# Small products of the first mixer issued in one visit of the array, modulation weights by two chunks

## The chip, the cores and the metric

The kernel runs on one core of a Trainium2 chip. The metric is the device time in microseconds of one execution. Before the change three runs took 1012.62, 1013.31 and 1016.01 us; the median is 1013.31. Engines are named as in the profile: PE is the matrix engine, DVE the vector engine, ACT the scalar engine, SP the queue that issues most loads.

## The reference, cut to what matters

One inference step of a two-layer transformer-like trunk over 384 tokens (128 context tokens, 256 latent tokens) of width 1024. Each layer computes six modulation vectors from a conditioning vector, then a mixer, then a feed-forward network. The change concerns the mixer of layer 0:

```
mod = silu(cond) @ w_mod[l] + b_mod[l]            # 1024 -> 6 x 1024: shift, scale, gate, twice
u   = layer_norm(x) * (1 + sc1) + sh1
# mixer of layer 0: projections of u, then
#   windowed attention, 8 query heads on 2 key/value heads:
s = q @ k^T / 8, masked;  p = softmax([s, sink]);  wo = p @ v
#   bidirectional retention, 8 heads (rv: values, s0: a state from the cache):
o = (q k^T * decay) @ rv + (q * decay) @ s0
x = layer_norm(ALPHA * x + g1 * ([ret, wo] @ w_out))
```

The feed-forward network behind it (1024 to 2816 and back) takes most of the time and isn't touched.

## The kernel before, in words

Everything is in float32; large products run as three products of rounded and rest parts (`r_...`, `l_...` for weights, `ur`, `ul` for activations). Weight tiles of 512 KB are loaded by the SP queue into a ring of five raw tiles (`raw_unit`, line 162), then ACT copies the rounded part and DVE subtracts for the rest part (`split`, line 172). The modulation weights use the same ring but no split: PE multiplies them straight from the raw tile.

The tokens are tiled by 128 (`NB` = 3 blocks). The first mixer consists of projections in slabs (`rqk`, `rvg`, each a stretch of 128 by 512 matmuls), twelve window items (three blocks by four head pairs), the retention of two halves, and modulation steps 2, 3 and 4 of layer 0. A string of steps (`AORDER`, line 33) sets the order in which the code emits these; a scheduler then places instructions on each engine by priority and by when it takes operands to be ready. `hmm` and `boost` (lines 116 and 120) raise the priority of a small product by 600, so it slips in between the matmuls of a projection as soon as its operand is due. `tc.issue_after(op)` adds an order edge only: what is emitted inside it comes behind `op` on its engine.

Three functions matter. `mod_pe` (line 223) takes eight chunks of the contraction. Each is one load `rawm` and four products, each on a column tile of 32 of the array. `win1` (line 855) makes the scores `ws` of an item and their exponentials `wp` for both heads (q = 0, 1). `win2` (line 884) normalises `wp`, transposes it on PE (`tw`), copies it on ACT (`wpT`), multiplies it with the values (`wpo`, six products for an item of blocks 1 and 2 and two for one of block 0, on column tiles of 64) and writes the rounded and rest parts (`catr` on ACT, `catl` on DVE, `cat_split`, line 388). `av_sample` (line 1044) is the retention's output: products of weights `at` with values `rv` and of `gm` with the state `s0`, accumulated in `po`. In the trace a product in float32 shows as two matmuls, so a chunk of modulation has eight and a long item's `wpo` twelve; `mod`, `wpo` and the other small products all carry line 118, a projection line 377.

A run of small products of one tile shape that PE takes without another shape between is called a visit here.

Of the kernel before, what the change touches and what calls it, by code (L numbers as in the profile page):

```python
# [19 lines left out]
P = 128  # L20
D = 1024
NB = 3
KC = 8
# [41 lines left out]
def trunk_kernel(ctx: ExitStack, tc: tile.TileContext, a: dict):  # L65
    nc = tc.nc
    mm = nc.tensor.matmul
    V, S, G, SY = nc.vector, nc.scalar, nc.gpsimd, nc.sync
# [41 lines left out]
    def big(shape, name):  # L110
        return perm.tile(shape, F32, tag="s", name=name, bufs=4)
# [4 lines left out]
    def boost(f, *args, **kw):  # L116
        with tc.high_priority(offset=BOOST):
            return f(*args, **kw)  # L118

    def hmm(*args, **kw):  # L120
        return boost(mm, *args, **kw)
# [13 lines left out]
    ident = const.tile([P, P], F32, name="ident")  # L135
# [11 lines left out]
    cmod = const.tile([P, KC, 32], F32, name="cmod")  # L147
# [14 lines left out]
    def raw_unit(src, shape, name):  # L162
        t = perm.tile([P] + shape, F32, tag="raw", name=name, bufs=5)
        SY.dma_start(t, src)
        return t
# [48 lines left out]
    def mod_tile(l, v):  # L214

        bm = perm.tile([P, 256], F32, tag="bm", name=f"bm{l}_{v}", bufs=2)
        if v in (2, 5):
            bsrc = a["b_mod"][l, v * D : (v + 1) * D].rearrange("(j n) -> j n", j=4)
            for j in range(4):
                S.dma_start(bm[32 * j : 32 * j + 32, :], bsrc[j : j + 1, :].broadcast_to([32, 256]))  # L220
        return bm

    def mod_pe(l, v, ps, hmm=hmm):
        w = a["w_mod"][l].rearrange("(p k) n -> p k n", k=KC)
        bm = mod_tile(l, v)
        for k in range(KC):
            t = raw_unit(w[:, k, v * D : (v + 1) * D], [D], f"rawm{l}_{v}_{k}")
            for j in range(4):
                hmm(ps[32 * j : 32 * j + 32, 0:256], cmod[:, k, :], t[:, j * 256 : (j + 1) * 256],
                    start=(k == 0), stop=(k == KC - 1))  # L230
        if v in (2, 5):
            V.tensor_tensor(bm, ps[:, 0:256], bm, ALU.add)
        else:
            V.tensor_copy(bm, ps[:, 0:256])
        return bm
# [146 lines left out]
    def transpose_to(dst, srcs, pt):  # L382
        n = len(srcs)
        for i, s_ in enumerate(srcs):
            boost(nc.tensor.transpose, pt[:, i * P : (i + 1) * P], s_, ident)
        S.copy(dst, pt[:, 0 : n * P].rearrange("p (n t) -> p n t", n=n))
# [431 lines left out]
    def mixer_ab(u, cat, early, early_es, ap, ap_es, pto, mt, gm, wkT, wv, wqT, mods):  # L818
# [15 lines left out]
        bk = Banks("pab", S=1, M=1, X=1)  # L834
# [3 lines left out]
        if True:  # L838
# [7 lines left out]
            s0 = big([P, 2, 4, P], "s0")  # L846
# [37 lines left out]
            def win2(b, c):  # L884
                nk = 1 if b == 0 else 3
                w = nk * P
                tiles = [0] if b == 0 else [1, 2, 3]
                kv = c // 2
                pts, es, sm = wst.pop((b, c))
                V.tensor_tensor(sm, sm, es, ALU.add)  # L890
                V.reciprocal(sm, sm)
                pTs = []
                for q, pt in enumerate(pts):
                    V.tensor_scalar(pt[:, 0:w], pt[:, 0:w], sm[:, q : q + 1], None, ALU.mult)
                    pT = ap2.tile([P, 3, P], F32, tag="pT", name=f"wpT{b}_{c}_{q}", bufs=5)
                    transpose_to(pT[:, 0:nk, :], [pt[:, i * P : (i + 1) * P] for i in range(nk)], (pto("T", f"tw{b}_{c}_{q}") if q == 0 else bk("X", f"tw{b}_{c}_{q}")))
                    pTs.append(pT)
                po = pto("O", f"wpo{b}_{c}")
                for i in range(nk):
                    for q in range(2):  # L900
                        hmm(po[64 * q : 64 * q + 64, 0:P], wv[:, tiles[i], kv * 64 : kv * 64 + 64], pTs[q][:, i, :],
                            start=(i == 0), stop=(i == nk - 1))
                cat_split(cat, 4 + c, 1, slice(b * P, (b + 1) * P), po[:, 0:P])

            items = [(b, c) for b in range(NB) for c in range(4)]
# [138 lines left out]
            def av_sample(hh, b, ats):  # L1044
                rv = half[hh][2]
                po = pto("O", f"po{hh}_{b}")
                ic = slice((b - 1) * P, b * P)
                for c in range(2):
                    for r_ in range(2):
                        hmm(po[:, 256 + c * P : 256 + (c + 1) * P], gm[hh][:, c, r_, ic], s0[:, r_, 2 * hh + c, :],  # L1050
                            start=(r_ == 0), stop=(r_ == 1))
                    for q in (2 * c, 2 * c + 1):
                        for ji in range(2):
                            hmm(po[:, q * 64 : q * 64 + 64], ats[q][:, ji, ic], rv[:, 1 + ji, q * 64 : q * 64 + 64],
                                start=(ji == 0), stop=(ji == 1))
                return ret_out(hh, b, po)

            def ret_core(hh):
# [285 lines left out]
    for l in range(2):  # L1344
        pto = Banks(f"pto{l}", T=1, O=1)
# [32 lines left out]
        hh = tuple(lnp.tile([P, NHEAD, NTOK], F32R, name=f"hh{q}{l}") for q in "rl")  # L1378
# [142 lines left out]
```

## Time and profile before

| | |
|---|---|
| median of three runs | 1013.31 us |
| the profiled execution | 1011.62 us |
| its span, first to last instruction | 1009.8 us |
| PE busy | 990.1 us, 98 % of the span, 5679 matmuls |
| DVE busy | 636.3 us, 63 % |
| ACT busy | 432.4 us, 43 % |
| stretch of the first mixer's window items, modulation and retention | about 73 to 210 us of the span |

Busy time of PE is modelled from the start of a matmul, and matmuls are pipelined: a row that lasts 0.40 us may be followed by the next row after 0.23. What a matmul costs PE is therefore read as the distance from its start to the next start. Rows of one shape that follow each other are merged into one row with their count. In the timeline, "idle before" names what ended a wait, if PE stood.

### The profile page before, as it was taken

Reading aid. Unit: us, or ns where it says so; the run is one execution under the profiler, and the core shown is the slowest. Engines: PE = TensorE matmul, PEld = TensorE weight load, DVE = VectorE, ACT = ScalarE, POOL = GpSimd, SP = SyncE. Lnnn points to the kernel's source line nnn. Section 1 sums busy time; section 2 is a strip of 40 time slices with the busy share of each in tenths; the row PEclk is TensorE's granted clock in tenths of the full one; section 3 lists DMA queues with packets and bytes.
Section 4 is the critical chain, followed back from the end, with each engine's and each line's share of the span. In section 5 each row is a group of like instructions: output and inputs, shape, how many; then the busy total and the mean of one; then the engine's idle time right before and its main releaser. Section 6 shows DMA issues by size and latency. Waiting matters only on the chain.

```text
span 1009.8 us, 14877 instructions
## 1 busy us (share of the span) xinstructions
PE 990.1 (98%) x5679; PEld 826.9 (82%) x5679; DVE 636.3 (63%) x1338; ACT 432.4 (43%) x786; POOL 1.2 (0%) x5
## 2 busy tenths in 40 slices
PE   9999999999999999999999999999999999999996
PEld 4775566688898988989987766787899999999985
DVE  5487658588795967968557577568743333335554
ACT  3395533227543333333427556554743333333410
POOL 0000000000000000000000000000000000000000
PEclk9999999999999999999999999999999999999999
DMA  9975446473896767777624333235574444444401
GB/s 304 300 204 189 148 147 196 168 255 95 281 304 219 215 212 248 220 219 226 193 83 151 99 95 94 91 122 211 180 265 145 125 124 126 123 124 126 155 21 43
DMA packets 109704, 172.86 MB, mean 171 GB/s; under 512 B 10176, under 2 KB 78272, under 8 KB 109632
## 3 DMA queue, kind: packets, MB, share of 16 engines
q1 hardware_dynamic: 106960, 170.87, 53.4%
q10 hardware_dynamic: 2672, 1.04, 0.4%
q8 instruction: 45, 0.74, 0.3%
q14 instruction: 27, 0.22, 0.1%
HBM read 167.52 MB, written 4.36 MB: 170 GB/s over the span
## 4 chain that ended last, share of the span: by engine, by line
PE 87%; DVE 5%; DMA 3%; ACT 3%; issue 1%; SPq 0%; ACTq 0%; DVEq 0%
PE dn L518 17%; PE wg L542 17%; PE wu L542 16%; PE cd L377 7%; PE wo L377 5%; PE rvg L377 4%; PE s L377 2%; PE rqk L377 2%; PE hg L377 2%; PE mod L118 2%; PE hu L377 1%; DMA rawm<-in_w_mod 1%; PE ms L118 1%; PE wpo L118 1%; PE ws L118 1%
## 5 line engine op out<-in xcount | busy, mean ns | idle before, releaser
L542 PE MATMUL wg<-ulf,r_wg 128*128 128x384 f32 x320 | 108.4, 339 | 0.0
L542 PE MATMUL wg<-urf,r_wg 128*128 128x384 f32 x320 | 108.0, 339 | 0.3 <-DVE sg L559 0.3
L542 PE MATMUL wu<-ulf,r_wu 128*128 128x384 f32 x320 | 108.2, 338 | 0.0
L542 PE MATMUL wu<-urf,r_wu 128*128 128x384 f32 x320 | 108.1, 339 | 0.0
L542 PE MATMUL wu<-urf,l_wu 128*128 128x384 f32 x320 | 108.1, 338 | 0.0
L542 PE MATMUL wg<-urf,l_wg 128*128 128x384 f32 x320 | 108.1, 338 | 0.0
L249 DVE SCALAR_TENSOR_TENSOR z<-mraw,cs,z 128x1024 f32<-128x1024 f32 x70 | 86.2, 1281 | 9.2 <-DMA mraw<-in_w_mod 8.8
L175 DVE TENSOR_TENSOR l_wg<-raw_wg,r_wg 128x1024 fp32r<-128x1024 f32 x40 | 48.7, 1224 | 67.9 <-ACT r_wg L173 67.8
L175 DVE TENSOR_TENSOR l_wd<-raw_wd,r_wd 128x1024 fp32r<-128x1024 f32 x36 | 44.1, 1225 | 53.6 <-ACT r_wd L173 53.6
L173 ACT CAST r_wd<-raw_wd 128x1024 fp32r<-128x1024 f32 x36 | 37.8, 1050 | 88.4 <-PE wu L542 40.1
L175 DVE TENSOR_TENSOR l_wu<-raw_wu,r_wu 128x1024 fp32r<-128x1024 f32 x40 | 48.6, 1223 | 39.5 <-ACT r_wu L173 39.5
L173 ACT CAST r_wg<-raw_wg 128x1024 fp32r<-128x1024 f32 x40 | 42.0, 1049 | 72.1 <-PE dn L518 29.9
L173 ACT CAST r_wu<-raw_wu 128x1024 fp32r<-128x1024 f32 x40 | 42.0, 1050 | 62.5 <-issue 23.9
L518 PE MATMUL dn<-l_wd,hr 128*128 128x512 f32 x168 | 66.6, 396 | 0.0
L518 PE MATMUL dn<-r_wd,hr 128*128 128x512 f32 x168 | 66.5, 396 | 0.0
L518 PE MATMUL dn<-r_wd,hl 128*128 128x512 f32 x168 | 66.5, 396 | 0.0
L542 PEld LDWEIGHTS wg<-urf,r_wg 128*128 128x128 f32 x320 | 60.1, 188 | 2.3 <-issue 0.8
L542 PEld LDWEIGHTS wu<-urf,r_wu 128*128 128x128 f32 x320 | 60.1, 188 | 1.6 <-ACT r_wg L173 0.8
L542 PEld LDWEIGHTS wu<-ulf,r_wu 128*128 128x128 f32 x320 | 60.1, 188 | 0.5
L542 PEld LDWEIGHTS wg<-ulf,r_wg 128*128 128x128 f32 x320 | 60.1, 188 | 0.5
L542 PEld LDWEIGHTS wg<-urf,l_wg 128*128 128x128 f32 x320 | 60.1, 188 | 0.0
L542 PEld LDWEIGHTS wu<-urf,l_wu 128*128 128x128 f32 x320 | 60.1, 188 | 0.0
(418 smaller groups left out, 2168.6 us busy)
## 6 DMA issues: line engine op xcount, KB each, us to landing
raw_wd<-in_w_down SPq DMA_DIRECT2D x44, 512.0 KB
rawm<-in_w_mod SPq DMA_DIRECT2D x40, 512.0 KB
mraw<-in_w_mod SPq DMA_DIRECT2D x40, 512.0 KB
raw_wg<-in_w_gate SPq DMA_DIRECT2D x40, 512.0 KB
raw_wu<-in_w_up SPq DMA_DIRECT2D x40, 512.0 KB
raw_cd<-in_w_in_cd SPq DMA_DIRECT2D x20, 512.0 KB
ms<-in_w_mod SPq DMA_DIRECT2D x16, 512.0 KB
raw_rqk<-in_w_in_ab SPq DMA_DIRECT2D x16, 256.0 KB
```

What stands on the lines that cost most here:

```text
L118: return f(*args, **kw)
L173: S.copy(r, t)
L175: V.tensor_tensor(lo, t, r, ALU.subtract)
L249: V.scalar_tensor_tensor(z[c], t, cs[:, c, k : k + 1], z[c], ALU.mult, ALU.add)
L377: op = mm(ps[:, col : col + width], u[pu][:, k0 + kk, b * P : (b + 1) * P], (r, lo)[pw][:, kk, :], start=(first and i == 0 and pu + pw == ...
L518: mm(acc[b, nh], h[fc][ph][:, b * P : (b + 1) * P], wrl[pw][:, nh * 512 : (nh + 1) * 512], start=(fc == 0 and ph + pw == 0), stop=(last an ...
L542: mm(ps[j][:, 0:NTOK], un[i][pw][:, k, j * P : (j + 1) * P], u2[pu][:, 4 * i + k, :], start=(i == 0 and k == 0 and pu + pw == 0), stop=(i ...
```

## The change

`mod_pe` takes chunks in pairs: both loads are issued, then the four products of the second chunk come first and the four of the first chunk behind them (an order edge after the last). `win2` normalises both heads' exponentials first; the transposes of q = 1 go ahead of those of q = 0, and an order edge ties the latter behind; the copies follow in that order; the products of the item are chained one behind the other. `av_sample` emits the products with the values first, from q = 3 down, chained, and those with the state behind them. The arithmetic is the same but for the order of some sums. `mw` (the steps 5 of both layers, in the output phase) uses `mod_pe` too.

```diff
--- before.py
+++ after.py
@@ -223,11 +223,18 @@
     def mod_pe(l, v, ps, hmm=hmm):
         w = a["w_mod"][l].rearrange("(p k) n -> p k n", k=KC)
         bm = mod_tile(l, v)
-        for k in range(KC):
-            t = raw_unit(w[:, k, v * D : (v + 1) * D], [D], f"rawm{l}_{v}_{k}")
-            for j in range(4):
-                hmm(ps[32 * j : 32 * j + 32, 0:256], cmod[:, k, :], t[:, j * 256 : (j + 1) * 256],
-                    start=(k == 0), stop=(k == KC - 1))
+        for k0 in range(0, KC, 2):
+            ts = [raw_unit(w[:, k, v * D : (v + 1) * D], [D], f"rawm{l}_{v}_{k}") for k in (k0, k0 + 1)]
+
+            def chunk(n):
+                for j in range(4):
+                    op = hmm(ps[32 * j : 32 * j + 32, 0:256], cmod[:, k0 + n, :], ts[n][:, j * 256 : (j + 1) * 256],
+                             start=(k0 == 0 and n == 1), stop=(k0 == KC - 2 and n == 0))
+                return op
+
+
+            with tc.issue_after(chunk(1).ins):
+                chunk(0)
         if v in (2, 5):
             V.tensor_tensor(bm, ps[:, 0:256], bm, ALU.add)
         else:
@@ -889,17 +896,28 @@
                 pts, es, sm = wst.pop((b, c))
                 V.tensor_tensor(sm, sm, es, ALU.add)
                 V.reciprocal(sm, sm)
-                pTs = []
                 for q, pt in enumerate(pts):
                     V.tensor_scalar(pt[:, 0:w], pt[:, 0:w], sm[:, q : q + 1], None, ALU.mult)
+
+                pTs = {}
+                behind = nullcontext()
+                for q in (1, 0):
                     pT = ap2.tile([P, 3, P], F32, tag="pT", name=f"wpT{b}_{c}_{q}", bufs=5)
-                    transpose_to(pT[:, 0:nk, :], [pt[:, i * P : (i + 1) * P] for i in range(nk)], (pto("T", f"tw{b}_{c}_{q}") if q == 0 else bk("X", f"tw{b}_{c}_{q}")))
-                    pTs.append(pT)
+                    tp = pto("T", f"tw{b}_{c}_{q}") if q == 0 else bk("X", f"tw{b}_{c}_{q}")
+                    with behind:
+                        for i in range(nk):
+                            op = boost(nc.tensor.transpose, tp[:, i * P : (i + 1) * P], pts[q][:, i * P : (i + 1) * P], ident)
+                    S.copy(pT[:, 0:nk, :], tp[:, 0 : nk * P].rearrange("p (n t) -> p n t", n=nk))
+                    behind = tc.issue_after(op.ins)
+                    pTs[q] = pT
                 po = pto("O", f"wpo{b}_{c}")
+                behind = nullcontext()
                 for i in range(nk):
                     for q in range(2):
-                        hmm(po[64 * q : 64 * q + 64, 0:P], wv[:, tiles[i], kv * 64 : kv * 64 + 64], pTs[q][:, i, :],
-                            start=(i == 0), stop=(i == nk - 1))
+                        with behind:
+                            op = hmm(po[64 * q : 64 * q + 64, 0:P], wv[:, tiles[i], kv * 64 : kv * 64 + 64], pTs[q][:, i, :],
+                                     start=(i == 0), stop=(i == nk - 1))
+                        behind = tc.issue_after(op.ins)
                 cat_split(cat, 4 + c, 1, slice(b * P, (b + 1) * P), po[:, 0:P])
 
             items = [(b, c) for b in range(NB) for c in range(4)]
@@ -1045,14 +1063,18 @@
                 rv = half[hh][2]
                 po = pto("O", f"po{hh}_{b}")
                 ic = slice((b - 1) * P, b * P)
-                for c in range(2):
-                    for r_ in range(2):
-                        hmm(po[:, 256 + c * P : 256 + (c + 1) * P], gm[hh][:, c, r_, ic], s0[:, r_, 2 * hh + c, :],
-                            start=(r_ == 0), stop=(r_ == 1))
-                    for q in (2 * c, 2 * c + 1):
-                        for ji in range(2):
-                            hmm(po[:, q * 64 : q * 64 + 64], ats[q][:, ji, ic], rv[:, 1 + ji, q * 64 : q * 64 + 64],
-                                start=(ji == 0), stop=(ji == 1))
+                behind = nullcontext()
+                for q in range(3, -1, -1):
+                    for ji in range(2):
+                        with behind:
+                            op = hmm(po[:, q * 64 : q * 64 + 64], ats[q][:, ji, ic], rv[:, 1 + ji, q * 64 : q * 64 + 64],
+                                     start=(ji == 0), stop=(ji == 1))
+                        behind = tc.issue_after(op.ins)
+                with behind:
+                    for c in range(2):
+                        for r_ in range(2):
+                            hmm(po[:, 256 + c * P : 256 + (c + 1) * P], gm[hh][:, c, r_, ic], s0[:, r_, 2 * hh + c, :],
+                                start=(r_ == 0), stop=(r_ == 1))
                 return ret_out(hh, b, po)
 
             def ret_core(hh):
```

The order of instructions on PE shows the window item of block 2, head pair 2. `tw` are transposes, `wpo` the output products, `mod0_3` modulation step 3, `rvg0_1` a projection. Before:

```order
L118 MATMUL tw2_2_0_1579<-ident_69,wp2_2_0_1529 128x128 x3
L118 MATMUL tw2_2_1_1586<-ident_69,wp2_2_1_1531 128x128 x3
L377 MATMUL rvg0_1_1165<-r_rvg0_1_1102,ul0_91 128x512
L118 MATMUL wpo2_2_1591<-wpT2_2_0_1578,wv_648 64x128
L377 MATMUL rvg0_1_1165<-l_rvg0_1_1103,ur0_90 128x512
L118 MATMUL wpo2_2_1591<-wpT2_2_1_1585,wv_648 64x128
L118 MATMUL wpo2_2_1591<-wpT2_2_0_1578,wv_648 64x128
L118 MATMUL wpo2_2_1591<-wpT2_2_1_1585,wv_648 64x128
L118 MATMUL wpo2_2_1591<-wpT2_2_0_1578,wv_648 64x128
L118 MATMUL wpo2_2_1591<-wpT2_2_1_1585,wv_648 64x128
```

After the change, at the same item:

```order
L118 MATMUL tw2_2_1_1580<-ident_69,wp2_2_1_1531 128x128 x3
L118 MATMUL tw2_2_0_1586<-ident_69,wp2_2_0_1529 128x128 x3
L118 MATMUL mod0_3_1625<-rawm0_3_3_1641,cmod_82 32x256 x3
L118 MATMUL mod0_3_1625<-rawm0_3_2_1639,cmod_82 32x256 x4
L384 MATMUL rvg0_1_1165<-r_rvg0_3_1116,ul0_91 128x512
L118 MATMUL wpo2_2_1591<-wpT2_2_0_1585,wv_648 64x128
L118 MATMUL wpo2_2_1591<-wpT2_2_1_1579,wv_648 64x128
L118 MATMUL wpo2_2_1591<-wpT2_2_0_1585,wv_648 64x128
L118 MATMUL wpo2_2_1591<-wpT2_2_1_1579,wv_648 64x128
L118 MATMUL wpo2_2_1591<-wpT2_2_0_1585,wv_648 64x128
L118 MATMUL wpo2_2_1591<-wpT2_2_1_1579,wv_648 64x128
L384 MATMUL rvg0_1_1165<-l_rvg0_3_1117,ur0_90 128x512
```

The six products of `wpo` stood in two visits with a projection matmul between; they stand in one. The transposes of q = 1 have come ahead, and the modulation chunk behind the item has become a pair in front of it, the second chunk's products first.

On the SP queue, the loads of modulation step 4. In brackets are the engines and DMA rings whose semaphores an entry waits for. Before:

```order
L164 DMA rawm0_4_0_1810<-in_w_mod 128x1024 [waits DMAHW4_49,DMAHW1_49,DVE_49]
L164 DMA rawm0_4_1_1816<-in_w_mod 128x1024 [waits DMAHW6_49,DMAHW4_49,PE_49]
L164 DMA rawm0_4_2_1822<-in_w_mod 128x1024 [waits DMAHW7_49,DMAHW2_49,DVE_49]
L164 DMA rawm0_4_3_1828<-in_w_mod 128x1024 [waits DMAHW6_49,PE_49]
L164 DMA rawm0_4_4_1834<-in_w_mod 128x1024 [waits DMAHW7_49,PE_49]
L164 DMA rawm0_4_5_1840<-in_w_mod 128x1024 [waits DMAHW3_49,DVE_49]
L164 DMA rawm0_4_6_1846<-in_w_mod 128x1024 [waits DMAHW3_49,DMAHW0_49,PE_49]
L164 DMA rawm0_4_7_1852<-in_w_mod 128x1024 [waits DMAHW1_49,PE_49]
```

And after:

```order
L164 DMA rawm0_4_0_1810<-in_w_mod 128x1024 [waits DMAHW5_49,DMAHW1_49,DVE_49]
L164 DMA rawm0_4_1_1812<-in_w_mod 128x1024 [waits DMAHW6_49,DMAHW3_49,DVE_49]
L164 DMA rawm0_4_2_1822<-in_w_mod 128x1024 [waits DMAHW7_49,DMAHW6_49,PE_49]
L164 DMA rawm0_4_3_1824<-in_w_mod 128x1024 [waits DMAHW5_49,PE_49]
L164 DMA rawm0_4_4_1834<-in_w_mod 128x1024 [waits DMAHW2_49,DVE_49]
L164 DMA rawm0_4_5_1836<-in_w_mod 128x1024 [waits DMAHW4_49,DMAHW2_49,DVE_49]
L164 DMA rawm0_4_6_1846<-in_w_mod 128x1024 [waits DMAHW0_49,PE_49]
L164 DMA rawm0_4_7_1848<-in_w_mod 128x1024 [waits DMAHW4_49,DVE_49]
```

The order of the loads is the same; the engine that an entry waits for (DVE or PE) has changed for the chunks 1, 2, 4 and 7.

On PE, modulation step 4 among the matmuls of the projections `rqk1` and `rvg1`. Before, two chunks:

```order
L118 MATMUL mod0_4_1808<-rawm0_4_5_1840,cmod_82 32x256 x4
L377 MATMUL rqk1_2_1970<-r_rqk1_3_1309,ur0_90 128x512
L377 MATMUL rqk1_2_1970<-r_rqk1_3_1309,ul0_91 128x512
L377 MATMUL rqk1_2_1970<-l_rqk1_3_1310,ur0_90 128x512
L377 MATMUL rvg1_0_2046<-r_rvg1_0_1685,ur0_90 128x512
L377 MATMUL rvg1_0_2046<-r_rvg1_0_1685,ul0_91 128x512
L118 MATMUL mod0_4_1808<-rawm0_4_6_1846,cmod_82 32x256 x4
```

After, the third pair:

```order
L384 MATMUL rvg1_0_2046<-l_rvg1_1_1693,ur0_90 128x512
L384 MATMUL rvg1_0_2046<-r_rvg1_1_1692,ur0_90 128x512
L118 MATMUL mod0_4_1808<-rawm0_4_5_1836,cmod_82 32x256 x4
L118 MATMUL mod0_4_1808<-rawm0_4_4_1834,cmod_82 32x256 x4
L118 MATMUL trqk1_2_2071<-ident_69,t1rqk1_2_1995 128x128 x4
L384 MATMUL rvg1_0_2046<-r_rvg1_1_1692,ul0_91 128x512
```

A chunk stood alone between projection matmuls, five of them from the next; a pair now stands in one piece, the second chunk first.

## Rows read from the trace of the kernel before

**Rows 1.** The page: the span, the engines' busy time, the chain that ended last.

```profile
span 1009.8 us, 14877 instructions
...
PE 990.1 (98%) x5679; PEld 826.9 (82%) x5679; DVE 636.3 (63%) x1338; ACT 432.4 (43%) x786; POOL 1.2 (0%) x5
...
PE 87%; DVE 5%; DMA 3%; ACT 3%; issue 1%; SPq 0%; ACTq 0%; DVEq 0%
```

**Rows 2.** The view of waits, PE: total us, times, longest.

```profile
PE mod L118 <- DMA rawm<-in_w_mod: 1.5, 3, 0.8
```

**Rows 3.** Timeline of PE, step 4: start us, duration, instruction, count, idle before.

```profile
172.49 0.40 PE L377 MATMUL rqk<-r_rqk,ul 128*128 128x512 f32 x1
172.81 0.64 PE L118 MATMUL mod<-rawm,cmod 128*32 128x256 f32 x8
173.38 0.50 PE L377 MATMUL rqk<-l_rqk,ur 128*128 128x512 f32 x1
173.72 0.39 PE L377 MATMUL rqk<-r_rqk,ur 128*128 128x512 f32 x1
173.95 0.39 PE L377 MATMUL rqk<-r_rqk,ul 128*128 128x512 f32 x1
...
177.73 0.64 PE L118 MATMUL mod<-rawm,cmod 128*32 128x256 f32 x8 [0.83 <-DMA rawm<-in_w_mod]
```

**Rows 4.** Timeline of PE, two window items of block 2 and their scores.

```profile
116.53 0.92 PE L118 MATMUL ws<-wkT,wqT 64*128 64x384 f32 x4
...
117.50 0.83 PE L118 MATMUL tw<-ident,wp 128*128 128x128 f32 x6
...
118.62 0.43 PE L118 MATMUL wpo<-wpT,wv 128*64 128x128 f32 x2
118.98 0.49 PE L377 MATMUL rvg<-r_rvg,ul 128*128 128x512 f32 x1
119.41 0.87 PE L118 MATMUL wpo<-wpT,wv 128*64 128x128 f32 x10
120.20 0.64 PE L118 MATMUL mod<-rawm,cmod 128*32 128x256 f32 x8
...
121.20 0.92 PE L118 MATMUL ws<-wkT,wqT 64*128 64x384 f32 x4
...
123.47 1.07 PE L118 MATMUL wpo<-wpT,wv 128*64 128x128 f32 x12
124.47 1.06 PE L118 MATMUL mod<-rawm,cmod 128*32 128x256 f32 x14
```

**Rows 5.** Timeline of PE, modulation step 5 in the output phase.

```profile
250.56 1.07 PE L229 MATMUL mw<-rawm,cmod 128*32 128x256 f32 x16
251.56 0.44 PE L118 MATMUL ht<-ident,hsg 128*128 128x128 f32 x2
```

**Rows 6.** Timeline of DVE beside the same window item.

```profile
115.71 0.29 DVE L392 TENSOR_TENSOR catl<-wpo,catr 128x128 fp32r<-128x128 f32 x1
...
116.11 0.75 DVE L894 TENSOR_SCALAR wp<-wp,wsm 128x384 f32<-128x384 f32 x2
...
120.61 0.29 DVE L392 TENSOR_TENSOR catl<-wpo,catr 128x128 fp32r<-128x128 f32 x1 [0.20 <-ACT catr L391]
```

**Rows 7.** Timeline of ACT beside the same window item.

```profile
118.09 0.86 ACT L386 COPY wpT<-tw 128x384 f32<-128x384 f32 x2 [2.41 <-PE tw L118]
```

**Rows 8.** The chain of waits, step 4: start us, us, what, count.

```profile
158.62 5.01 DMA rawm<-in_w_mod
164.37 3.87 DMA rawm<-in_w_mod
...
171.17 1.23 DVE l_rvg L175
172.42 5.26 DMA rawm<-in_w_mod
```

**Rows 9.** The view of waits, the SP queue.

```profile
SPq L164 <- PE mod L118: 24.7, 15, 5.8
```

## The prediction

> **What bounds the kernel now.** I read the page first. The reader is to see there that TensorE is busy for 990.1 of the span's 1009.8 us and that the chain that ended last lies on PE for 87 % [rows 1]. Then I read the view of waits for PE. What concerns the changed lines is one row: PE waited for a modulation chunk three times, 1.5 us in all [rows 2]. So PE is short of time, not of operands, and the change can gain only by what it takes off PE's own stream, and lose by what it makes PE wait for. The third view is PE's timeline at three places, read from start to start, since the ends of matmuls are modelled. There the small products of the first mixer stand between 512-wide matmuls of the projections, and entering and leaving them costs more than the matmuls themselves. The last view is DVE's and ACT's timeline beside it, for the operands of the small products.
>
> **What a visit costs.** Two neighbouring 512-wide matmuls start 0.23 us apart (173.72 and 173.95) [rows 3]. When the next thing is a product on another tile of the array, its start comes 0.32 us behind the matmul's (172.49 to 172.81) [rows 3], or 0.43 us where a semaphore is waited for as well (118.98 to 119.41) [rows 4]: an entry costs 0.09 to 0.20 us. The first matmul after a visit needs 0.34 us to the next start (173.38 to 173.72) instead of 0.23 [rows 3]: a return costs 0.11. The visit itself has a fixed part too. Two matmuls of the window output (a product is two in the trace) take 0.36 us (118.62 to 118.98), ten take 0.79 (119.41 to 120.20), twelve take 1.00 (123.47 to 124.47) [rows 4]: split 2 and 10 they take 0.15 more than together. One chunk of modulation, 8 matmuls, takes 0.57 us (172.81 to 173.38) [rows 3], two chunks, 16 matmuls, take 1.00 (250.56 to 251.56) [rows 5]: apart 0.14 more than together.
>
> A visit saved is thus worth 0.14 or 0.15 inside, 0.09 to 0.20 at the entry and 0.11 at the return: 0.34 to 0.46 us. Where the visit stood directly behind another small one, there is no return to save and the value is 0.23 to 0.35.
>
> The Trainium skill puts this differently: "TensorEngine Tiling (Array Packing)", Key Properties, says that a change of tiling mode drains TensorE, and "TensorE: Matmul & The Clock Gate", Single matmul latency, gives 128 cycles for a drain. An estimate from it is 53 ns at 2.4 GHz, twice per visit, 0.11 us for a visit saved and 2.2 us for the 21 visits counted below. The trace agrees that a switch costs, but shows about three times as much per visit; the rows decide here, and what the smaller figure would give is the fourth rival.
>
> **The change part by part.**
>
> Modulation by two chunks. Steps 2, 3 and 4 of the first mixer hold 24 chunks. In the order of the instructions these make 25 visits before and 14 after (a chunk or a pair is here and there broken by another product): 11 fewer.
>
> Window output. The 112 matmuls of the 12 items stand in 19 visits before (eight of 2, three of 4, six of 10, two of 12) and in 12 after (four of 4, eight of 12): 7 fewer.
>
> Scores of the mixer, which tile the array by 64 rows, fall from 41 visits to 38 because the order around them moved: 3 fewer.
>
> Together 21 fewer. The returns to a projection's matmul fall from 58 to 44, by 14, so 14 visits are worth 0.34 to 0.46 and 7 are worth 0.23 to 0.35: 4.8 to 6.4 plus 1.6 to 2.5, together 6.4 to 8.9 us. The entries without a wait are the more frequent, so I take a value nearer the lower end, 7.1 us.
>
> av_sample: its products, those on attention weights and those on the state, all use the whole 128 by 128 array, and they were a contiguous stretch already. No visit is saved; I count nothing, with 0.2 us either way as the bound (one entry with a wait for each of the four calls, less what they show now: nothing). The transposes of the window items, q=1 before q=0, and the second normalisation moved ahead of the first transposes are the same instructions; their price is a wait and is counted next.
>
> What becomes later. First, the grouped window output needs both copies. Follow one item: the subtraction into the concatenated tile at 115.71, normalisation of both halves from 116.11 for 0.75 [rows 6], so 1.15 us after 115.71; about 0.1 to the transposes; 0.59 from the first transpose (117.50) [rows 4] to the copies (118.09), which take 0.86 [rows 7]; 0.1 to the products; 1.00 for their twelve matmuls [rows 4]; 0.4 from their end (120.20) [rows 4] to the next subtraction (120.61) [rows 6]. The sum is 4.2 us, while the period is 4.67 now (scores at 116.53 and 121.20) [rows 4], set by PE. After the change PE needs some 0.4 to 0.7 less per item, that is 4.0 to 4.3. The loop of latencies is therefore just level with PE, and ahead of it in the items without a modulation pair: I estimate three waits of a third of a microsecond, 1.0 us. The bounds are 0 (the loop hides) and 0.47 for each of eight items, 3.8 us (the period stays 4.67).
>
> Second, the pairs. The ring of raw tiles has five places. The load of a pair's second chunk, which PE now wants first, is queued on SP behind the first's. In step 4 the queue's entries wait mostly in pairs for DVE or for PE, where these alternated before. A load needs 3.9 us from its issue to PE's start on it with the queue otherwise empty (164.37) and 5.3 with others in flight (172.42) [rows 8]; SP waits for PE's modulation 15 times now, 24.7 us in all [rows 9]. A pair takes PE 1.0 us, and as the matmuls between them add up in the new order, pairs follow each other after 3 to 6 us in step 4 and 2.8 to 4.2 us in step 2. With half as many meetings between PE and a load, step 4 should wait less than now (0.83 us at 177.73 [rows 3] is the largest of its three named stalls): of the 1.5 us I count 1.0 as gone. Step 2, which has no named stall, should wait about 1.0 us. All new waits together, 1.0 of the window loop, 1.0 of step 2 and 1.0 gone in step 4, make 1.0 us. The bounds are 1.5 gained (the row of waits goes and nothing comes) and 12.9 lost (second rival).
>
> The Trainium skill has a rule that speaks against both edits: "TensorE: Matmul & The Clock Gate", The mechanism, says that matmuls run strictly in order. By that rule a product put first whose operand is late holds all behind it. The trace agrees: at 177.73 PE stood 0.83 us before a modulation visit with projection matmuls behind it [rows 3].
>
> The sum: 7.1 saved less 1.0 waited, 6.1 us. The profiled execution took 1011.62 us, its span 1009.8 and 1.8 around it. 1011.62 - 6.1 = 1005.5. The median of the runs shown, 1013.31, lies 1.69 above the profiled execution, so the time on the scale of the runs is 1007.2 us. The bounds of the forecast's own case are 1004.3 (8.9 saved, no new wait: 1013.31 - 8.9 is 1004.4, and a little noise) and 1010.2 (6.4 saved, 3.3 waited, the just visible gain).
>
> **The rivals.**
>
> First rival, the window loop keeps its period: PE leaves the visits earlier and waits for ACT's copies or DVE's normalisation instead. For it: 4.2 us of latency against 4.0 to 4.3 of need. Against it: it would have to be 0.4 us longer than I add up. Price 3.8 us for the eight long items, and with the 1.0 of step 2: 7.1 - 3.8 - 1.0 = 2.3 gained, 1011.0 us, which is within 0.3 % (3.04 us, about what a measurement of this kernel can tell from no change).
>
> Second rival, the pairs starve PE, the result slower than before. The mechanism: in steps 2 and 4 the load of a pair's second chunk is issued only when PE has freed the place of an earlier pair, its trip of 3.9 to 5.3 us [rows 8] is longer than the spacing of pairs, and PE stands with the projection behind it. At a spacing of 2.8 us each of the eight pairs waits 4.6 - 2.8 = 1.8, in sum 14.4; less today's 1.5 these are the 12.9 lost. Against 7.1 saved that is 5.8 us slower, 1019.1 us. It decides from (7.1 + 1.5) / 12 = 0.7 us per pair over all twelve. For it speaks that the queue waits on PE's modulation already [rows 9]; against it that only three such waits reach PE now [rows 2], that the ring holds two pairs, and that most spacings are over 3 us.
>
> Third rival, step 4 gives half back. Three loads of step 4 lie on the chain, the last of them behind a split on DVE [rows 8]; if they stay bound to the splits, and these to loads that come no earlier, PE arrives sooner and waits. Price half of 7.1, with the 1.0 of waits: 2.6 gained, 1010.7 us. Against it: the splits wait for loads whose places PE and DVE free, and these come earlier together with PE.
>
> Fourth rival, a visit saved is worth only its inside, 0.15 us, because the entry and the return beside it move to another place of the stream: 21 x 0.15 = 3.2, less 1.0 waited, 2.2 gained, 1011.1 us. The Trainium skill's figures for a drain (the two pages above) come out near that, 2.2 less 1.0. Against it: 14 returns are gone by count.
>
> That the change does not do what it says is excluded for the visits by the order of the instructions; for the time it is what the first and third rival say.
>
> **How the numbers follow.** The forecast's case has 0.68, the first rival 0.13, the third 0.08, the fourth 0.04 and the second 0.07. The first, third and fourth end within 0.3 %, the second slower: faster 0.68, within 0.25, slower 0.07. The predicted time is the forecast's, 1007.2. Its own range is 1004.3 to 1010.2. The range for 8 in 10 starts at 1004.3 and reaches over the first, third and fourth rival to 1013.0; outside lie the second rival and a tenth for terms that are beyond my bounds.
>
> **What would show it.** Right: visits of twelve window matmuls and of sixteen modulation matmuls in PE's timeline, each with 1.00 us to the next start; scores of consecutive window items 4.2 to 4.4 us apart; PE's busy time about 6 us shorter while the waits named for modulation stay under 3 us; the first matmul of the output projection about 6 us earlier. The FFN stretches behind should keep their lengths. Wrong: scores still 4.6 us apart with PE waiting for the copies, or waits for modulation loads above 7 us in total, or an unchanged start of the output projection with earlier scores.

## The result and the profile after

The changed kernel took 1005.41 us (median of 5 runs, 1004.18 to 1008.77), the kernel before 1013.31 in the same set. The ratio is 0.9925, with the 95 % interval 0.9911 to 0.9939, a gain of 6 to 9 us. Two further sets gave 0.9928 (0.9916 to 0.9941) and 0.9937 (0.9921 to 0.9953). The median of the sixteen runs is 1006.1 us. The forecast was 1007.2 with the range 1004.3 to 1013.0.

The page of the changed kernel, the rows that answer to [rows 1], then its view of waits for PE, which answers to [rows 2] (total us, times, longest):

```profile
span 1003.6 us, 14858 instructions
...
PE 982.0 (98%) x5679; PEld 825.8 (82%) x5679; DVE 636.0 (63%) x1338; ACT 431.0 (43%) x786; POOL 1.2 (0%) x5
...
PE 87%; DVE 4%; DMA 4%; ACT 3%; issue 1%; SPq 0%; ACTq 0%; DVEq 0%
```

```profile
PE mod L118 <- DMA rawm<-in_w_mod: 2.7, 4, 1.1
...
PE tw L118 <- DVE wp L900: 0.6, 3, 0.3
```

PE is busy for 8.1 us less with the same 5679 matmuls, and the span is 6.2 us shorter. PE waits for chunks 1.2 us more. So the gain is in PE's own stream, and a part of it is paid back in waits.

PE's timeline at window items of block 2, the stretch of [rows 4] (start, duration, instruction, count, idle before):

```profile
108.31 0.92 PE L118 MATMUL ws<-wkT,wqT 64*128 64x384 f32 x4
...
110.64 0.40 PE L384 MATMUL rvg<-r_rvg,ur 128*128 128x512 f32 x1
110.97 0.88 PE L118 MATMUL wpo<-wpT,wv 128*64 128x128 f32 x12
111.77 0.62 PE L118 MATMUL mod<-rawm,cmod 128*32 128x256 f32 x2
112.32 0.92 PE L118 MATMUL ws<-wkT,wqT 64*128 64x384 f32 x4
...
113.61 0.85 PE L118 MATMUL tw<-ident,wp 128*128 128x128 f32 x6 [0.16 <-DVE wp L900]
...
115.81 0.88 PE L118 MATMUL wpo<-wpT,wv 128*64 128x128 f32 x12
...
117.27 0.92 PE L118 MATMUL ws<-wkT,wqT 64*128 64x384 f32 x4
...
121.15 0.92 PE L118 MATMUL ws<-wkT,wqT 64*128 64x384 f32 x4
...
122.45 0.84 PE L118 MATMUL tw<-ident,wp 128*128 128x128 f32 x6 [0.17 <-DVE wp L900]
```

A long item's twelve output matmuls stand in one row and take 0.80 us to the next start (110.97 to 111.77). Before, items in two visits took 0.36 and 0.79 besides the matmul between, and an unbroken visit took 1.00 [rows 4]. The entry from a projection's matmul takes 0.33 us here (110.64 to 110.97), where it took 0.43 at 119.41 [rows 4]; of the seven long items entered so, five show 0.33 or 0.34 and two 0.42 or 0.43. Scores start at 108.31, 112.32, 117.27 and 121.15: 4.3 us apart in the mean, instead of 4.67 [rows 4]. Of the long items' transposes two wait 0.16 and 0.17 us for the normalisation; that is the latency loop showing. The longest of the three waits in the view, 0.3, stands ahead of the first short item.

Modulation step 4, the stretch of [rows 3], its last three pairs:

```profile
168.66 1.07 PE L118 MATMUL mod<-rawm,cmod 128*32 128x256 f32 x16
...
172.19 1.07 PE L118 MATMUL mod<-rawm,cmod 128*32 128x256 f32 x16
173.19 0.66 PE L118 MATMUL trqk<-ident,t1rqk 128*128 128x128 f32 x4
...
176.33 1.07 PE L118 MATMUL mod<-rawm,cmod 128*32 128x256 f32 x16 [1.10 <-DMA rawm<-in_w_mod]
177.33 0.70 PE L118 MATMUL rs<-rqk 64*128 64x256 f32 x4
```

Sixteen matmuls of a pair take 1.00 us. The last pair waits 1.10 us for its load; before, the longest wait here was the 0.83 of the sixth single chunk [rows 3]. The chain of waits of the changed kernel shows that load's trip, 6.5 us, and above it those for the last pairs of steps 2 and 3, which answers to [rows 8]:

```profile
91.75 5.68 DMA rawm<-in_w_mod
...
130.94 5.51 DMA rawm<-in_w_mod
...
169.78 6.50 DMA rawm<-in_w_mod
176.33 1.07 PE mod L118 x16
```

It begins at 169.78, 0.1 us after the pair that starts at 168.66 is through. The load just ahead of it in the queue had waited 0.7 us for that pair to free a place in the ring. The other two are queued behind a pair of their step in the same way.

The first mixer ends where the output projection begins. That matmul is at 202.62 in the kernel before and at 194.90 in the changed one, first fence before, second after:

```profile
202.62 0.40 PE L377 MATMUL wo<-r_wo,catr 128*128 128x512 f32 x1
```

```profile
194.90 0.40 PE L384 MATMUL wo<-r_wo,catr 128*128 128x512 f32 x1
```

7.7 us are gained there, and 6.2 at the end of the span. Behind it two things differ: the modulation steps 5, which use `mod_pe` too, and two products of the retention output, which now stand behind the first `wo` and take 0.3 us with them. The last matmul of the program starts 797.9 us behind the first of the output projection in the profiled execution of before; in the changed kernel it was 799.4, 799.7 and 799.5 us in three profiles, and in the kernel with only the window part, whose order of PE's instructions behind is that of before, 798.9. So the profiled execution of before was a short one behind the mixer, as it was 1.7 us below the median. The runs' medians lie 7.9, 7.3 and 6.1 us apart in the three sets; the spans' 6.2 is at the low end of that. The mixer's length repeats within 0.1 us in three profiles of the changed kernel and is the surer number for what the change does.

### The profile page after: what moved, and what is told of

It is laid out like the page before. It is cut to its first block, busy times and chain, and to the rows that moved or that the text cites. A ratio compares the mean times of both kernels' runs of the same rounds, so it can differ in the third digit from the quotient of the medians.

```text
span 1003.6 us, 14858 instructions
## 1 busy us (share of the span) xinstructions
PE 982.0 (98%) x5679; PEld 825.8 (82%) x5679; DVE 636.0 (63%) x1338; ACT 431.0 (43%) x786; POOL 1.2 (0%) x5
## 4 chain that ended last, share of the span: by engine, by line
PE 87%; DVE 4%; DMA 4%; ACT 3%; issue 1%; SPq 0%; ACTq 0%; DVEq 0%
PE dn L525 17%; PE wu L549 17%; PE wg L549 17%; PE cd L384 7%; PE wo L384 6%; PE rvg L384 3%; PE rqk L384 2%; PE s L384 2%; DMA rawm<-in_w_mod 2%; PE hg L384 2%; PE hu L384 1%; PE ms L118 1%; PE po L118 1%; PE mod L118 1%; PE idle L129 1%; PE mw L231 1%
## 5 line engine op out<-in xcount | busy, mean ns | idle before, releaser
L173 ACT CAST r_wd<-raw_wd 128x1024 fp32r<-128x1024 f32 x36 | 37.8, 1050 | 86.6 <-PE wu L549 40.4
```

The costliest lines, as they stand in the source:

```text
L173: S.copy(r, t)
```

## The experiments

I use two numbers throughout: the length of the first mixer, from the first start of `rqk` to the first start of `wo` in the profiled execution, and how often the order of instructions changes the array's tile in that stretch. Counted strictly between those two matmuls every count is lower by three; only differences are used. The granted clock of the stretch is 1.00 in every profile. Waits by name, below, are all of PE's waits in it that the timeline names, those for chunks and the others. In kernels with the changed retention output the mixer is 0.3 us shorter by the two products that moved out.

| kernel | changes of tile | first mixer, us | waits for chunks, us | median, us | ratio (95 %) |
|---|---|---|---|---|---|
| before | 119 | 143.9 | 1.5 | 1013.3 to 1013.5 | 1 |
| changed | 80 | 136.0 | 2.7 | 1005.4 | 0.9925 (0.9911 to 0.9939) |
| changed, again | 80 | 135.9 | 2.2 | 1006.1 | 0.9928 (0.9916 to 0.9941) |
| changed, third | 80 | 135.9 | 2.5 | 1007.2 | 0.9937 (0.9921 to 0.9953) |
| modulation only | 101 | 140.6 | 1.4 | 1010.5 | 0.9960 (0.9945 to 0.9976) |
| window only | 106 | 140.4 | 2.0 | 1009.5 | 0.9958 (0.9942 to 0.9974) |
| retention only | 120 | 144.1 | 1.7 | 1012.8 | 0.9994 (0.9979 to 1.0009) |
| first chunk first | 107 | 139.2 | 1.2 | 1007.9 | 0.9939 (0.9922 to 0.9957) |
| chain without order | 101 | 141.8 | 2.0 | 1010.0 | 0.9966 (0.9954 to 0.9978) |
| visit broken inside | 106 | 143.4 | 1.8 | 1013.9 | 1.0004 (0.9992 to 1.0016) |
| same work beside | 88 | 140.2 | 2.3 | 1010.5 | 0.9972 (0.9961 to 0.9983) |
| four chunks | 72 | 136.9 | 3.7 | 1007.9 | 0.9964 (0.9941 to 0.9987) |
| four in step 2 only | 76 | 136.4 | 2.3 | 1008.1 | 0.9942 (0.9929 to 0.9955) |

The theory: each change of tile has a price on PE, about 0.20 us with the measured sum, and the change gains by having fewer. The rivals: the loads, queued in pairs, come earlier; or only the time at which operands are ready matters.

### The parts alone

Three kernels take one of the three changed functions each from the diff above and leave the others as before.

> Only the modulation by pairs; window output and retention output as before. In the order of instructions from the first mixer's projections to the output projection, changes of array tile fall from 119 to 101 (the whole change: 80). Theory, a price per change of tile: the whole change took 6.2 us off the profiled span and brought about 1.6 us of new waits, so 7.8 over 39 changes of tile, 0.20 us each; here 18 x 0.20 = 3.6, less 1.2 of waits for chunks, 2.4 us faster than before, ratio 0.9976. Rival, the gain is that loads are queued in pairs and come earlier: then most of it is here, 5 us or more, ratio 0.995 or less, and the kernel that pairs the loads but not the products keeps it too.

> Only the window item part (normalisation, transposes, output products in one visit); modulation chunk by chunk as before. Changes of tile 119 to 106. Theory, a price per change of tile: 13 x 0.20 = 2.6, less 0.4 of waits in the window loop, 2.2 us faster, ratio 0.9978, visits of twelve window matmuls in the timeline. Rival, loads in pairs: no gain, ratio 1.000.

> Only the retention output's order (products with the values first, those with the state behind). Changes of tile 119 to 120. Theory, a price per change of tile: no difference, ratio 1.000 within 0.001. Rival, that the order of operands by readiness pays by itself there: up to 1 us faster, ratio 0.999.

Modulation alone gives 3.0 us in the medians (3.3 in the mixer), window items alone 4.0 (3.5), the retention output nothing clear of noise (0.7 in the medians, 0.2 longer in the mixer). Both gains are larger than expected by 0.6 and 1.8 us. For the modulation, 18 x 0.20 = 3.6 accounts for its 3.3 in the mixer. For the window items 13 x 0.20 = 2.6 doesn't account for 3.5, and less so since waits by name grew by 0.9 us there: PE's own stream is 4.4 us shorter, 2.9 of it inside the window output. What is missing is told with the inside of the window output below. The parts sum to 6.6 us in the mixer, the whole is 7.9: the parts alone remove 18 and 13 changes of tile, together 39. That this is because a visit that stays whole also lets its neighbours stand together is likely, not shown.

### The loads in pairs, the products not

```diff
-            with tc.issue_after(chunk(1).ins):
-                chunk(0)
+            with tc.issue_after(chunk(0).ins):
+                chunk(1)
```

(and `start` and `stop` with the first and last chunk accordingly). The loads are queued as in the changed kernel.

> The whole change, but in each pair the first chunk's products go first and the second's behind them. The loads are queued in pairs as in the changed kernel; the modulation products stand in 26 visits (14 in the changed kernel), since the first chunk is ready before the second and other work slips between; changes of tile 107. Theory, a price per change of tile: 12 x 0.20 = 2.4, about as the window part alone, 2 to 2.5 us faster than before, ratio 0.9977, and some 5 us slower than the changed kernel. Rival, loads in pairs: as the changed kernel, 6 to 8 us faster, ratio 0.993.

The ratio is 0.9939 and the mixer 139.2 us. The median is 5.6 us below that of before, where the theory had 2 to 2.5; it lies nearer to the rival's expectation, 1.9 us above the changed kernel's three sets, not 5, and the intervals overlap. So the runs' times don't part this kernel from the changed one; the mixer does. Of PE's timeline in step 4:

```profile
169.84 0.64 PE L118 MATMUL mod<-rawm,cmod 128*32 128x256 f32 x8
170.41 0.51 PE L384 MATMUL rqk<-l_rqk,ur 128*128 128x512 f32 x1
...
172.31 0.64 PE L118 MATMUL mod<-rawm,cmod 128*32 128x256 f32 x8 [0.48 <-DMA rawm<-in_w_mod]
172.88 0.50 PE L384 MATMUL rqk<-r_rqk,ul 128*128 128x512 f32 x1
```

Chunks stand alone again, 0.57 us each. Of the mixer's gain 3.2 us are lost against the changed kernel with the same queue of loads, so paired loads alone don't keep it. But the kernel is 1.2 us better in the mixer than the window part alone, with one change of tile more. 0.3 of this are the two products that moved out and 0.6 are fewer waits by name (2.4 against 3.0; for chunks 1.2 against 2.0, in one profile each). The rest stays open, and whether paired loads help a little isn't settled.

### What makes the visit in the window items

```diff
+                behind = nullcontext()
                 for i in range(nk):
                     for q in range(2):
-                        hmm(po[64 * q : 64 * q + 64, 0:P], ...
+                        with behind:
+                            op = hmm(po[64 * q : 64 * q + 64, 0:P], ...
+                        behind = tc.issue_after(op.ins)
```

The kernel is the whole change with this piece alone in `win2`: the transposes run q = 0 first as before.

> The whole change, but in the window items only the chaining of the output products is kept: normalisation, transposes and copies go head by head with q = 0 first, as before. The operand ready last, the copy of q = 1, is then wanted second. In the order of instructions the output stands in 19 visits again (12 in the changed kernel), changes of tile 101 (80). Theory, the order by readiness makes the visit and the visit is the gain: as the modulation part alone, 3 to 4 us faster than before, ratio 0.9965, 3.5 to 4.5 us slower than the changed kernel. Rival, the chain alone suffices or the earlier normalisation matters: within 1 us of the changed kernel.

The theory held against the kernel before: 0.9966, 3.3 us faster. Against the changed kernel of the same set it is 2.7 us slower in the medians, less than expected, and 5.9 in the mixer (141.8 us). The mixer is 1.2 us longer than with modulation alone; waits by name are 3.6 us against 2.1. In PE's timeline the visits are broken as before:

```profile
118.09 0.43 PE L118 MATMUL wpo<-wpT,wv 128*64 128x128 f32 x2
118.46 0.49 PE L384 MATMUL rvg<-r_rvg,ur 128*128 128x512 f32 x1
118.88 0.87 PE L118 MATMUL wpo<-wpT,wv 128*64 128x128 f32 x10
119.68 0.50 PE L384 MATMUL rvg<-r_rvg,ul 128*128 128x512 f32 x1
...
122.84 1.07 PE L118 MATMUL wpo<-wpT,wv 128*64 128x128 f32 x12
123.84 1.06 PE L118 MATMUL mod<-rawm,cmod 128*32 128x256 f32 x14
```

Two matmuls on the copy that is ready first, a projection matmul, then the ten others; and where nothing stands between, 1.00 us for the twelve (122.84 to 123.84) as before. Built the other way round, with the transposes of q = 1 first and no chain on the products, the order of PE's instructions is that of the changed kernel row for row. Built with the chain and the earlier normalisation, but the transposes of q = 0 first, it is that of the kernel above row for row. Neither was run. So neither the chain nor the earlier normalisation changes the order of PE's instructions here; the order of the transposes does. What makes the visit is that the products begin with the operand that comes last: when it is there, all are. ACT's copies show it, first for the unbroken visit of before that begins at 123.47 [rows 4], then for the changed kernel's at 110.97:

```profile
122.76 0.86 ACT L386 COPY wpT<-tw 128x384 f32<-128x384 f32 x2 [2.18 <-PE tw L118]
```

```profile
110.05 0.86 ACT L910 COPY wpT<-tw 128x384 f32<-128x384 f32 x2 [1.88 <-PE tw L118]
```

Before, the second copy ends at 123.62, 0.15 us after the visit has begun; after, at 110.91, 0.06 ahead of it.

### The price of a broken visit

Both kernels add to every window item one 128 by 128 transpose whose result isn't used, once behind the first output product, once ahead of it:

```diff
+                xt = tp
                 po = pto("O", f"wpo{b}_{c}")
...
                         behind = tc.issue_after(op.ins)
+                        if i == 0 and q == 0:
+                            with behind:
+                                op = boost(nc.tensor.transpose, xt[:, 384:512], pts[0][:, 0:P], ident)
+                            behind = tc.issue_after(op.ins)
```

```diff
+                xt = tp
+                with behind:
+                    op = boost(nc.tensor.transpose, xt[:, 384:512], pts[0][:, 0:P], ident)
                 po = pto("O", f"wpo{b}_{c}")
```

> The changed kernel with one more 128 by 128 transpose per window item, its result unused, placed inside the window output, behind its first product: each of the twelve visits is broken in two. Changes of tile 106. Its twin does the same extra work directly ahead of the output. Theory, a price per change of tile: 18 changes more than the twin at 0.20 us, 3.6 us slower than the twin (bounds 2.8 to 5.5 from 12 visits at 0.23 to 0.46). Rival, that what pays is only when the operands are ready and not the unbroken visit: the twins are equal within 0.7 us, since both wait for the same operands.

> The changed kernel with the same extra transpose per window item, its result unused, placed ahead of the window output, so that the visits stay whole. Changes of tile 88. Theory, a price per change of tile: twelve transposes at 0.11 us and 8 changes at 0.20, 2.9 us slower than the changed kernel, that is 4 to 5 us faster than before, ratio 0.9955, and 3.6 us faster than the twin. Rival: as the twin.

The twins are 3.4 us apart in the medians and 3.1 in the mixer, for 18 changes of tile: 0.17 to 0.19 us per change. In the second kernel one long item's visit is broken all the same, by modulation (2 matmuls at 96.58, 10 at 97.94), so eleven visits differ and not twelve: 0.28 to 0.31 us each. Waits by name are 1.0 us shorter in the kernel with the break inside (3.1 against 4.1). Without them the twins are 4.1 us apart, and 3.9 of this lie in the window output itself: 0.36 us per visit. In the timelines, first with the break inside, then with the transpose beside:

```profile
119.58 0.43 PE L118 MATMUL wpo<-wpT,wv 128*64 128x128 f32 x2
119.95 0.33 PE L118 MATMUL tw<-ident,wp 128*128 128x128 f32 x1
120.20 0.87 PE L118 MATMUL wpo<-wpT,wv 128*64 128x128 f32 x10
121.00 0.92 PE L118 MATMUL ws<-wkT,wqT 64*128 64x384 f32 x4
```

```profile
117.39 0.33 PE L118 MATMUL tw<-ident,wp 128*128 128x128 f32 x1
117.65 0.88 PE L118 MATMUL wpo<-wpT,wv 128*64 128x128 f32 x12
118.45 0.92 PE L118 MATMUL ws<-wkT,wqT 64*128 64x384 f32 x4
```

The broken item takes 0.36 + 0.26 + 0.80 = 1.42 us from its first matmul, the whole one 0.26 + 0.80 = 1.06 with the same transpose: 0.36 us. The operands are the same and no wait is named in either, so this is the visit and not a wait. A short item loses the same: four matmuls take 0.37 us in the changed kernel, two take 0.36.

```profile
74.14 0.44 PE L118 MATMUL wpo<-wpT,wv 128*64 128x128 f32 x4
74.51 0.51 PE L384 MATMUL rqk<-r_rqk,ur 128*128 128x512 f32 x1
```

These rows say why a break costs. The products of q = 0 and q = 1 lie on two column tiles and run side by side, so the time goes by turns of the array and not by matmuls: two or four matmuls are one turn, 0.36 or 0.37 us, and ten or twelve are three, 0.80. Broken into 2 and 10 the twelve take four turns. Modulation shows the same: two matmuls of a chunk take 0.55 us (111.77 to 112.32), all eight 0.57 [rows 3]. So the price per change of tile isn't one number: the mixer gives 0.18 us for modulation alone, 0.27 for the window items alone and 0.39 for the kernel with the first chunk first.

The kernel with the transpose beside is 2.9 us faster than before, not 4 to 5, and 4.2 us longer in the mixer than the changed one, where 2.9 were expected for twelve transposes and eight changes. From start to next start the transposes take 2.9 us more (0.24 each, not 0.11), modulation, with one more broken visit, 0.5, the broken window visit 0.4 and waits by name 0.3.

### More chunks in one stretch

```diff
-        for k0 in range(0, KC, 2):
...
+        for k0 in range(0, KC, 4):
...
+            op = chunk(4 - 1)
+            for n in range(4 - 2, -1, -1):
+                with tc.issue_after(op.ins):
+                    op = chunk(n)
```

> The changed kernel with modulation by four chunks instead of two: four loads, then sixteen products in one stretch, the last chunk first. Changes of tile 72 against 80. If only changes of tile counted: 8 x 0.20 = 1.6 us faster than the changed kernel. But the ring of raw tiles has five places, so a four and the next do not fit together, and PE wants the last load of four first. Theory with the ring: each second four of the three steps waits 2 to 3 us for loads, waits for chunks rise from 2.7 to 8 us or more, 3 to 6 us slower than the changed kernel, ratio to before 0.996 to 0.999.

```profile
PE mod L118 <- DMA rawm<-in_w_mod: 3.7, 4, 2.0
```

Waits for chunks rise to 3.7 us, less than expected, and the mixer is 0.9 to 1.0 us longer than in the changed kernel although there are eight changes of tile fewer. In the medians it is 1.7 us slower than the changed kernel of the same set. The direction held in the mixer; the size of 3 to 6 us was far too large. That the ratio of 0.9964 lies in the expected range is luck: the seven runs scatter from 1006.5 to 1014.2 us. Since step 2 went without a wait, a further kernel takes four there alone (`range(0, KC, 4)` for step 2, 2 for the others):

> The changed kernel, but with four chunks in one stretch in modulation step 2 alone, where four at a time met no wait for loads when every step went by four; steps 3 and 4 stay by two. Changes of tile 76 against 80. Theory, price per change of tile and no new wait: 4 x 0.20 = 0.8 and up to 0.6 of waits that step 2 has now, 0.8 to 1.4 us faster than the changed kernel, ratio to before 0.9915. Rival, the loads of step 3 and of the slabs behind are pushed back: equal or up to 2 us slower than the changed kernel.

No gain is seen: 0.9942 beside 0.9937 of the changed kernel in the same set, a mixer of 136.4 against 135.9. Its step 2 waits nowhere, but step 3 waits 0.25 and 1.02 us for loads and 0.61 behind a window item. In sum the waits for chunks are no longer than the changed kernel's in this set (2.3 against 2.5), and all waits by name are 0.5 us longer; where the rest of the expected 0.8 us went stays open. No version better than the changed kernel came of it.

The changed kernel was run again in the set of the twins and the fours, and in that of the chain and of the fours in step 2:

> The changed kernel itself, as the yardstick of this call. All theories: 6 to 9 us faster than before, ratio about 0.9925, changes of tile 80.

> The changed kernel once more, as the yardstick of this call: ratio to before about 0.9927.

The two gave 0.9928 and 0.9937.

## Why the prediction was right, and where it was not

The forecast of 1007.2 lies at the upper edge of what the three sets gave (1005.4 to 1007.2); the gain of 6.1 was up to 1.8 us too small. The mechanism held: PE's own stream became shorter, and waits took a part of it back. Read from each matmul's start to the next over the first mixer, with the waits by name apart, the first profile shows where the time went (us):

| | before | changed |
|---|---|---|
| matmuls of the projections, with the entries behind them and the returns | 77.6 | 74.2 |
| window output | 10.8 | 7.9 |
| modulation | 15.7 | 13.1 |
| everything else | 37.8 | 37.0 |
| waits by name | 2.1 | 3.8 |

PE's own stream is 9.6 us shorter, where the sum had 7.1 and at most 8.9 (0.3 of the 9.6 are the two products that moved out), and the waits took 1.7 where it had 1.0. Both terms were too small and they have opposite signs; that the total came so near is in part luck.

- **Count of visits.** Held. The timeline has one row of twelve for each long item, four of four for the short ones, and pairs of 16 in modulation. Step 3's pairs are twice broken into 2 and 14 by scores.
- **Price of a visit.** Forecast 0.34 to 0.46 us, or 0.23 to 0.35 without a return. Too low in the sum: PE's 9.6 us, or 9.3 without the products that moved out, are 0.46 or 0.44 us for each of the 21 visits, where the 7.1 made 0.34. The twins measured 0.36 for the inside alone, where the sum had 0.14 or 0.15. The entries and returns were to bring 3.4 to 5.7 us; the matmuls of the projections show 3.4. The opening remark that entering and leaving cost more than the matmuls themselves isn't in the rows: 0.20 to 0.31 us for both there, against 0.36 to 1.00 for a visit's matmuls.
- **The inside of the window output.** This is the term of the sum that was mis-sized. I took 1.00 us for twelve matmuls in one visit, from a visit of before that was unbroken but began with the operand that was ready first. It came as 0.80. For the 112 matmuls this makes 10.8 us before, 9.5 as forecast and 7.9 measured (eight visits at 0.81 and four at 0.37): 1.6 us more than forecast, and about what a count of changes leaves open for the window items alone (4.4 less 2.6). The rows had a sign of it that I passed over: ten matmuls took 0.79 us, so 1.00 for twelve asked for a reason. Most of the entries fell as well, from 0.43 to 0.33; that this is a second wait that PE no longer meets is not shown.
- **The waits.** Forecast 1.0 us net; by name PE waited 1.6, 1.1 and 1.7 us longer than before in the three profiles, for chunks (2.7, 2.2 and 2.5 against 1.5) and for the window items' normalisation (0.6, 0.6 and 1.0 against 0.2). The place was partly wrong. Step 2 should have waited 1.0 and did so for 0.6, 0 and 0.5 in three profiles; step 3's last pair, of which I said nothing, waited 1.0, 0.9 and 0.4; step 4 should have fallen from 1.5 to 0.5 and had 1.1, 1.3 and 1.6. The last pair of a step is the one whose load waits for a place that a pair before it frees; in the first profile these trips took 5.5 to 6.5 us, where I had 3.9 to 5.3.
- **av_sample at nothing.** Held: 0.9994, with an interval that holds 1.
- **The stretches behind keep their length.** Not contradicted: 799.4 to 799.7 us, where 797.9 and 798.9 stand for the code of before. Whether the last 0.5 us are the change or scatter can't be told.
- **The first rival**, the window loop at its old period, fell: 4.3 us between scores. In the long items the loop is felt only as the two waits of 0.16 and 0.17. **The second**, pairs that starve PE, is a real mechanism but a small one with pairs: step 4's last pair at 1.1 to 1.6 us and step 3's at 0.4 to 1.0; with fours it takes more than the fewer changes of tile give. **The third** fell, since the output projection begins 7.7 us earlier. **The fourth**, that entry and return only move to another place, fell: the matmuls of the projections take 3.4 us less from start to start.

The drain of the Trainium skill ("TensorE: Matmul & The Clock Gate", Single matmul latency) would have made 0.11 us of a visit as an estimate. The twins don't agree: they show 0.36 for the inside alone, one more turn of the array. The same page, The mechanism, says that products on different tiles of the array overlap, starting some 4 ns apart. The trace agrees on what follows from it: read singly, output matmuls of q = 0 and q = 1 start 0.007 us apart in the visits of 0.80, and in the unbroken visit of before the first of q = 1 starts 0.20 us behind the first of q = 0 and the pairs stay apart by 0.02 or 0.09 to the end, so the visit takes 1.00.

## What to carry to other kernels

Where an engine runs small products between large ones, count the changes of shape in the order of its instructions, and price them from start to start in the timeline, entry, inside and return. Where the products lie on several column tiles, count the turns of the array: a broken visit can need one more. To keep a group whole it is not enough to tie its members: let it begin with the operand that comes last, so that nothing in it has to wait. Stop enlarging the group when its loads no longer fit into the buffers beside the next one's; here, with four chunks of a ring of five, the waits took more than the fewer visits gave.

## What was not expected of the hardware

Twelve matmuls on two column tiles take 0.80 us when both operands are there at the start and 1.00 when the second operand's wait falls behind the first product, in one unbroken visit, though the wait itself is over after 0.2 us: a pair that starts out of step stays so. And the same code behind the mixer took 797.9 us in the profile of the kernel before and 798.9 in that of the kernel with the window part alone: a single pair of profiles tells a difference of 6 us only to about 1.
